# Three rounded products for the gated linear attention's far part, with its splits placed anew, and the last head's first gated sum ahead of two splits

## The chip, the cores and the metric

The kernel runs on one core of a Trainium2 chip. The metric is device time in microseconds of one execution; the time before is 752.98 us, the median of three runs (752.88 to 753.81). The profile shows five engines: PE (matrix products into PSUM; its weight loads are shown as PEld), DVE and ACT (elementwise work from PSUM and SBUF), POOL (elementwise work from SBUF) and SP (issues DMAs). Each engine works through its instructions in a fixed order and waits at an instruction until its inputs are there and the buffer it writes is free.

## The reference

One block of a model on 512 tokens of width 1024, in fp32: a root-mean-square norm, one wide projection, a gated linear attention of four heads (GLA), an attention of eight heads with low-rank queries and keys (MLA), a gated sum of both, an output projection, and an MLP with squared ReLU. What the change touches first is GLA's recurrence over chunks of 64 tokens, forward and backward:

```python
    def step(state, inp):
        qc, kc, vc, dc = inp
        o = jnp.einsum('bhck,bhkv->bhcv', qc, state)
        state = state * dc[..., None] + jnp.einsum('bhck,bhcv->bhkv', kc, vc)
        return state, o
```

and second the gated sum `merged = sigmoid(z_ma) * y_gla + sigmoid(z_mb) * y_mla` ahead of `merged @ w_out`.

## The kernel before

**Number format.** A product of fp32 precision is made of three products of rounded values: each operand is split into a high part `hi` (rounded, written by ACT as a copy) and a low part `lo` (the operand less `hi`, written by DVE, or by POOL if `split` is told so; lines 91 to 94). `mm3` (lines 87 to 90) issues hi·hi, hi·lo and lo·hi into the same accumulator. A few products are still plain fp32 matmuls: GLA's scores, and line 742.

**GLA.** The 512 tokens are four tiles of 128. For head h, `gla_scores` makes the scores within a tile and between the two tiles of a half, and splits them and the transposed keys kT (lines 566 to 573). What crosses from one half of the sequence to the other goes through a matrix of 128 × 512: `gla_state` (line 574) multiplies keys by values for both halves in twelve rounded products, and ACT copies the accumulator to SBUF (`gla0s` to `gla3s`, line 584). `gla_out` (line 728) then adds, for each tile i of queries, the scores times the values and, at line 742, the queries `far[:, 0, i]` times the matrix of the other half: four fp32 matmuls, which the profile records as eight. The queries in `far` were multiplied by POOL in the head before (line 512, `across`). `gla_squares`, `gla_gated` and, a head later, `gla_turn` norm, gate and transpose the result; the transposes land in PSUM and ACT takes them from there at line 776 (`yg`).

**A head's loop.** Heads 0 to 2 run in one loop. Beside GLA of head h it makes the gates of head h+1 (`Gates`: scans and differences on DVE, exponentials on ACT, small copies on POOL), multiplies queries and keys by them (`within` on DVE, `across` on POOL) and projects queries and keys of head h+2; `begin_qk` loads and splits a weight (gq2, gk2, gq3, gk3), `finish_qk` multiplies. In head 2 it is the projections ckv1, zb4 and zb5 instead. Head 3 stands behind the loop, beside the start of MLA: `ckv_.sums` and `ckv_.diagonals` norm the compressed keys (lines 807 to 815; the power at line 809 is on POOL), `rotary_k` turns the shared key on DVE (krsin, kswap, kr, lines 894 to 897), `rotary_begin` (line 864) loads and splits two weights wr0 and wr1, `rotary_k_split` copies kr to kbuf on ACT, two tanh and two `yg` follow on ACT, and PE makes the rotary queries (`up_T`, tiles ro0 and ro1) from wr0 and wr1.

**PSUM.** Accumulators come from two rings of four buffers, "at" and "mm"; a tile takes the buffer of the tile four before it in its ring and waits until that has been read. In "mm" the transposes of two `yg`, the spread of ckv's factors, ro0 and ro1 follow one another.

**The end of MLA.** Head 7 of MLA is the last. `att_values` (step n of a loop over 37 steps) multiplies probabilities by values, half of the tokens at a time; `merge` (line 1150) forms (gate + 1) × av on DVE (tile `tb`), and POOL adds the GLA part (`my`, line 1153). For the last head `merge` is called once for each half, and the av products of the second half, which write the same accumulator, wait until the first half has been read. The output projection splits sums of pairs of merged heads: `split_first` (gao) and `split_sum` (glyo, glzo); for the third pair their low parts are on DVE at steps 34 to 36.

**Order.** Within each engine the order of work is the scheduler's, from the emitted order and its readiness, fixed in places by explicit order: POOL's from the GLA loop on follows the emitted order (`in_program_order`), PE's and that of ACT and DVE do in large stretches, and `goes_behind` sets one group behind another on given engines.

Of the kernel before, what the change touches and what calls it, by code (L numbers as in the profile page):

```python
# [56 lines left out]
def tile_block(ctx: ExitStack, tc: tile.TileContext, t, out: bass.AP):  # L57
# [10 lines left out]
    def u2(name, dt=F32, shape=(P, S)):  # L68
        return tl(list(shape), dt, "u2", 29, name)

    def u4(name, dt=F32R, shape=(P, 2, S)):
        return tl(list(shape), dt, "u4", 26, name)
# [19 lines left out]
    def split(hi, lo, src, rest=nc.vector):  # L92
        nc.scalar.activation(hi, src, AF.Copy)  # L93
        rest.tensor_tensor(lo, src, raw(hi), op=ALU.subtract)  # L94
# [479 lines left out]
    def gla_state(h, keys):  # L574

        half, at = h // 2, (h % 2) * GDV
        c = slice(at, at + GDV)
        acc = ps("at", f"gla{h}st")
        for j in range(NT):
            tok = slice(j * P, (j + 1) * P)  # L580
            mm3(acc[:, (j // 2) * GDV : (j // 2 + 1) * GDV], keys[:, 0, tok], keys[:, 1, tok],
                v[j, half][:, 0, c], v[j, half][:, 1, c], j % 2 == 0, j % 2 == 1)
        state = u2(f"gla{h}s")
        nc.scalar.activation(state, acc, AF.Copy)
        return state

# [138 lines left out]
    def gla_out(h, sc, state, far):  # L727

        half, at = h // 2, (h % 2) * GDV
        accs = [ps("at", f"gla{h}o{g}") for g in range(2)]  # L730
        c = slice(at, at + GDV)
        os = [accs[i // 2][:, (i % 2) * GDV : (i % 2 + 1) * GDV] for i in range(NT)]
        for i, o in enumerate(os):
            g = i // 2
            for x in range(2):
                j = 2 * g + x
                tok = slice(x * 256 + (i % 2) * P, x * 256 + (i % 2 + 1) * P)
                mm3(o, sc[g][:, 0, tok], sc[g][:, 1, tok], v[j, half][:, 0, c], v[j, half][:, 1, c],
                    i % 2 == 0 and x == 0, False, True)
        for i, o in enumerate(os):  # L740
            other = 1 - i // 2
            nc.tensor.matmul(
                o, far[:, 0, i], state[:, other * GDV : (other + 1) * GDV], start=False, stop=True,
                skip_group_check=True,
            )
        return os

    def gla_squares(h, os):
# [115 lines left out]
    def rotary_begin():  # L864
        res = []
        for x in range(2):
            wf = stage(3, P, f"wr{x}")
            lo = NOPE + x * HALF
            for k in range(3):
                nc.sync.dma_start(  # L870
                    wf[:, k, :].rearrange("p (h e) -> p h e", h=MH), w_uq[:, k, :, lo : lo + HALF]
                )
            wh, wl = halves(3, P, f"wr{x}")
            split(wh, wl, wf)
            res.append((wh, wl))
        return res

# [289 lines left out]
    def begin_qk(h, x):  # L1167
        col, name = ((C_GQ, "gq"), (C_GK, "gk"))[x]
        return begin(col + h * P, f"{name}{h}")
# [87 lines left out]
    for h in range(GH - 1):  # L1257
        sc, keys, far = gla_scores(*scaled_qk.parts())
        scaled_qk = Scaled(h + 1)
        gate = Gates(h + 1)  # L1260
        gate.logs()
        latent, j = ((cq_, 1), (cq_, 2), (ckv_, 0))[h]
        acc = latent.products(j)
        if h < 2:
            w_b, lows = begin_late(C_GQ + (h + 2) * P, f"gq{h + 2}")
        else:
            ckv_.begun[1], lows = begin_late(C_CKV + P, "ckv1")
        (rotary.angles, rotary.reduced, cq_.diagonals)[h]()
        gate.sums("f")
        state = gla_state(h, keys)  # L1270
        gate.exps("f")
        lows()
        latent.keep(j, acc)
        gate.sums("b")
        gate.exps("b")
        scaled_qk.within("f", gate.parts)
        scaled_qk.across("f", gate.parts)
        if j:
            latent.add_squares()
        if h:  # L1280
            gla_turn(h - 1)
        os = gla_out(h, sc, state, far)
        scaled_qk.within("b", gate.parts)
        rs = gla_squares(h, os)
        scaled_qk.across("b", gate.parts)
        if h < 2:
            w_k = begin_qk(h + 2, 1)
            gla_gated(h, os, rs)
            finish_qk(h + 2, 0, w_b)
            if h == 0:  # L1290
                cq_.begin(2)
            else:
                ckv_.begin(0)
                cq_.sums()
            finish_qk(h + 2, 1, w_k)
        else:
            zb = begin(C_ZB + 4 * P, "zb4")
            gla_gated(h, os, rs)
            cq_.spread()
            ckv_.keep(1, ckv_.products(1))  # L1300
            ckv_.add_squares()
            w_b = begin(C_ZB + 5 * P, "zb5")
            zb = proj_run(zb, xT)

    h = GH - 1
    sc, keys, far = gla_scores(*scaled_qk.parts())
    ckv_.sums()
    zb5 = proj_run(w_b, xT)
    cq = cq_.normed()
    cos, sin = rotary.tables()  # L1310
    state = gla_state(h, keys)
    late = [over_rms(acc, f"b{f}") for f, acc in ((4, zb), (5, zb5))]
    ckv_.diagonals()
    rotary_k()
    wr = rotary_begin()
    zb = begin(C_ZB + 6 * P, "zb6")
# [46 lines left out]
    for n in range(4 * MH + LAG_C - 1):  # L1363
        if n % 2 == 0 and 2 <= n <= 4 * MH:
            att_normalise((n - 2) // 4, (n - 2) % 4)
        scored = traced()
        if n < 4 * MH:
            att_scores(n // 4, n % 4)
            if n - 2 in flipping:
                goes_behind((scored, traced()), flipping[n - 2], SPLITTERS)  # L1370
        scored = scored, traced()
        if n == 0:
            goes_behind(scored, last_gate, PE_ONLY)
        if n == 3:
            span["fourth"] = scored
        if 2 <= n % 8 < 7:
            at = traced()
            next(units, None)
            if n == 2:
                gla_turn(GH - 1)  # L1380
            if n < 4:
                goes_behind((at, traced()), scored, PE_ONLY)
        if n in (6, 14):
            units = up_units(n // 8 + 2)
            at = traced()
            next(units)
            if n == 6:
                goes_behind((at, traced()), span["fourth"], SPLITTERS[:1])
        b = n - LAG_B
        if n == 30:  # L1390
            xs_ = wo_accs[1] = [ps("mm", f"wox{rb}") for rb in range(2)]
            at = traced()
            wo_product(1, ps_=(0,))
            begun = at, traced()
            goes_behind(begun, scored, PE_ONLY)
        if 0 <= b < 4 * MH:
            flips = traced()
            att_flip(b // 4, b % 4)
            flipping[n] = flips, traced()
            if n == 30:  # L1400
                goes_behind(flipping[n], begun, PE_ONLY)

        if n == 20:
            load_onto(B11, B12, w_out)
        extra = traced()
        for x, at in (("y", (18, 26, 34)), ("z", (20, 28, 36))):
            if n in at:
                p = at.index(n)
                to = (5, 6) if x == "y" else (7, 3)
                split_sum(wo_left[p], sums_of[p, x], *to, f"{x}o{p}", nc.gpsimd if p < 2 else nc.vector)  # L1410
        if n in (19, 30):
            p = (19, 30).index(n)
            split_first(wo_left[p], merged[p][0], f"o{p}", nc.gpsimd)
        if n < 4 * MH:
            goes_behind((extra, traced()), scored, SPLITTERS[:1])
        if n == 35:
            split_first(wo_left[2], merged[2][0], "o2")
        if n in (11, 13):
            streamed(1, B11, (n - 11) // 2)
            split_streamed(1, (n - 11) // 2)  # L1420
        if n in (21, 23):
            streamed(2, B21, (n - 21) // 2)
        if n == 15:
            load_w2(0, B11, w_out)
        if n == 17:
            at = traced()
            load_w2(0, B21, w_out, B22)
            span["sums"] = at, traced()
        if n == 23:
            load_onto(B21, B11, w_out)  # L1430
        if n == 24:
            load_w2(0, B12, w_out)
            load_w2(0, B22, w_out)
        c = n - LAG_C
        if c >= 0 and c % 2 == 1:
            att_values(c // 4, (c % 4) // 2)
        if n == 33:
            load_onto(B21, B12, w_out)
        if c > 0 and c % 8 == 7 and c // 8 < NP - 1:
            sums_of[c // 8, "y"], sums_of[c // 8, "z"] = merged_sums(c // 8, nc.gpsimd)  # L1440
# [334 lines left out]
```

## Time and profile before

| | |
|---|---|
| time, median of 3 runs | 752.98 us (752.88 to 753.81) |
| profiled execution | 753.01 us, span 751.0 us |
| granted clock of PE, mean | 0.999 |
| PE busy | 741.9 us, 99% of the span |
| DVE / ACT / POOL busy | 581.4 / 457.5 / 166.0 us |
| data moved by DMA | 88.90 MB, mean 118 GB/s |

A line of a timeline gives the start in us from the start of the span, the duration in us, the engine, the line of the kernel, the operation, the tile written and the tiles read, and the shape. `xN` joins N instructions of one form. A bracket at the end gives how long the engine had been idle before the instruction and what ended that. PE's matmuls overlap at their ends: their spacing is the time that one takes, not the duration shown. In the chain of work that ended last a line has start, length, engine and tile. L93 is the high part of a split and L94 its low part, L88 to L90 are the three products of `mm3`, whichever tile they are for.

### The profile page before, as it was taken

What the parts mean: (1) busy time and instruction counts of PE and PEld (TensorE: products, weight loads), DVE (VectorE), ACT (ScalarE), POOL (GpSimd) and SP (SyncE); (2) the same over time, 40 slices, a digit from 0 to 9 for tenths busy, and PEclk for the clock granted to TensorE, in tenths of its full rate; (3) what the DMA queues carried; (4) which work ended last, traced back from release to release, by engine and by line L of the source; (5) the groups of instructions that cost most, each with busy time, mean ns of one, the idle gap of its engine ahead of it and who ended that gap; (6) DMA issues with size and microseconds to landing.
All of it is one profiled execution on the core that took longest, in us unless ns stands there. A gap on an engine that the chain in (4) does not pass through costs nothing.

```text
span 751.0 us, 10202 instructions
## 1 busy us (share of the span) xinstructions
PE 741.9 (99%) x3688; PEld 628.3 (84%) x3688; DVE 581.4 (77%) x842; ACT 457.5 (61%) x776; POOL 166.0 (22%) x238
## 2 busy tenths in 40 slices
PE   9999999999999999999999999999999999999996
PEld 7888888888889888899888988888888888888885
DVE  7777886989787587888897688857696578747795
ACT  8556574686577476887956765435644464445644
POOL 0722110252672521246740100000000000000014
PEclk9999999999999999999999999999999999999999
DMA  9859582611222243459698321551226310640003
GB/s 309 266 128 231 175 175 84 113 29 29 84 57 39 40 92 102 109 145 249 196 226 245 107 67 30 168 169 56 57 85 196 113 57 21 203 141 0 29 0 113
DMA packets 94722, 88.90 MB, mean 118 GB/s; under 512 B 15792, under 2 KB 66992, under 8 KB 94672
## 3 DMA queue, kind: packets, MB, share of 16 engines
q1 hardware_dynamic: 88176, 75.64, 33.5%
q0 software_dynamic: 6208, 12.32, 9.2%
q8 instruction: 29, 0.48, 0.3%
q10 hardware_dynamic: 288, 0.28, 0.1%
q14 instruction: 21, 0.17, 0.1%
HBM read 83.25 MB, written 2.10 MB: 114 GB/s over the span
## 4 chain that ended last, share of the span: by engine, by line
PE 98%; DVE 1%; issue 0%; POOL 0%; ACT 0%; POOLq 0%
PE f L88 8%; PE f L89 8%; PE f L90 8%; PE gx L88 4%; PE gx L89 4%; PE gx L90 4%; PE first L330 3%; PE gz L88 2%; PE gz L89 2%; PE gz L90 2%; PE tp L1122 2%; PE zb L88 1%; PE zb L89 1%; PE zb L90 1%; PE s L88 1%; PE s L89 1%
## 5 line engine op out<-in xcount | busy, mean ns | idle before, releaser
L1714 POOL DMA_DIRECT2D gfin<-in_g_final x1 | 0.6, 628 | 284.0 <-PE f L90 284.0
L977 DVE TENSOR_TENSOR w<-w,w 128x1024 f32<-128x1024 f32 x32 | 38.7, 1220 | 0.3
L1102 DVE TENSOR_REDUCE top<-s 128x1 f32<-128x512 f32 x32 | 21.8, 683 | 5.6 <-PE s L90 5.5
L1107 ACT ACTIVATE e<-s,top 128x512 f32<-128x512 f32 x32 | 22.0, 687 | 4.1 <-DVE top L1102 3.1
L94 DVE TENSOR_TENSOR pT<-tp,pT 128x512 fp32r<-128x512 f32 x32 | 21.8, 682 | 2.4 <-ACT pT L93 2.0
L1452 DVE TENSOR_TENSOR h<-h,gx 128x512 f32<-128x512 f32 x32 | 21.5, 681 | 1.9 <-PE gx L90 1.8
L93 ACT ACTIVATE pT<-tp 128x512 fp32r<-128x512 f32 x32 | 19.0, 595 | 3.2 <-PE tp L1122 3.2
L88 PE MATMUL av<-pT,v 128*128 128x256 f32 x64 | 19.2, 300 | 0.9 <-DVE tb L1150 0.9
L1122 PE MATMUL tp<-ident,e 128*128 128x128 f32 x128 | 19.4, 274 | 0.0
L93 ACT ACTIVATE ghb<-y 128x512 fp32r<-128x512 f32 x16 | 10.1, 632 | 14.0 <-DVE y L923 14.0
L1518 ACT ACTIVATE fa<-f 128x512 f32<-128x512 f32 x32 | 18.5, 577 | 0.0
L90 PE MATMUL av<-pT,v 128*128 128x256 f32 x64 | 18.2, 284 | 0.0
L89 PE MATMUL av<-pT,v 128*128 128x256 f32 x64 | 18.1, 283 | 0.0
L1122 PEld LDWEIGHTS tp<-ident,e 128*128 128x128 f32 x128 | 15.2, 140 | 3.1 <-ACT e L1113 0.6
L93 ACT ACTIVATE b_00h<-w 128x1024 fp32r<-128x1024 f32 x7 | 7.4, 1060 | 12.6 <-PE gz L90 6.0
L562 ACT ACTIVATE bds<-bd 128x512 f32<-128x512 f32 x4 | 2.4, 597 | 20.5 <-PE bd L545 20.5
L93 ACT ACTIVATE b_10h<-w 128x1024 fp32r<-128x1024 f32 x7 | 7.4, 1059 | 12.1 <-PE gz L90 6.0
L93 ACT ACTIVATE b_20h<-w 128x1024 fp32r<-128x1024 f32 x7 | 7.4, 1059 | 12.1 <-PE gz L90 6.0
L973 POOL DMA_DIRECT2D w<-in_w_out x10 | 12.4, 1428 | 7.6 <-DVE bo60l L94 6.5
L88 PE MATMUL s<-kbuf,q 96*128 96x512 f32 x32 | 14.1, 439 | 0.0
L1527 ACT ACTIVATE px<-fa 128x256 f32<-128x256 f32 x32 | 13.4, 418 | 1.0
L646 POOL DMA_DIRECT2D gvw<-in_w_in x4 | 4.8, 1226 | 38.7 <-DVE gvw L651 34.0
(1769 smaller groups left out, 2920.0 us busy)
## 6 DMA issues: line engine op xcount, KB each, us to landing
w<-in_w_ff SPq DMA_DIRECT2D x64, 256.0 KB, 3.4
w<-in_w_out POOLq DMA_DIRECT2D x10, 512.0 KB, 9.3
grw<-in_w_in SPq DMA_DIRECT2D x8, 512.0 KB, 9.1
zaw<-in_w_in SPq DMA_DIRECT2D x8, 512.0 KB, 6.7
gvw<-in_w_in SPq DMA_DIRECT2D x8, 512.0 KB, 4.6
w<-in_w_out SPq DMA_DIRECT2D x16, 256.0 KB, 5.6
x<-in_xt SPq DMA_DIRECT2D x8, 256.0 KB, 5.2
vw<-in_w_first SPq DMA_DIRECT2D x8, 256.0 KB, 5.4
```

The lines of the kernel that those rows point to most:

```text
L88: nc.tensor.matmul(acc, lh, rh, start=start, stop=False, skip_group_check=onto)
L89: nc.tensor.matmul(acc, lh, rl, start=False, stop=False, skip_group_check=onto)
L90: nc.tensor.matmul(acc, ll, rh, start=False, stop=stop, skip_group_check=onto)
L93: nc.scalar.activation(hi, src, AF.Copy)
L94: rest.tensor_tensor(lo, src, raw(hi), op=ALU.subtract)
L330: nc.tensor.matmul(f_accs[i], a[:, i * P : (i + 1) * P], b, start=k == 0 and x == 0, stop=k == KD - 1 and x == 2)
L977: nc.vector.tensor_tensor(wq[dst][g], wq[x][g], wq[y][g], op=op)
L1102: nc.vector.tensor_reduce(top, acc, axis=AX.X, op=ALU.max, negate=True)
L1107: nc.scalar.activation(e, acc, AF.Exp, bias=top, accum_out=tot[:, qt % 2 : qt % 2 + 1])
L1122: nc.tensor.transpose(tp[:, k * P : (k + 1) * P], e[:, k * P : (k + 1) * P], ident)
L1452: nc.vector.tensor_tensor(hc, hc, acc, op=op)
L1518: nc.scalar.activation(a, acc, AF.Relu)
```

## The change

- **Far part of GLA.** `gla_state` returns a split matrix (hi by ACT, lo by DVE) in place of one copy. A new function `far_queries` splits the 128 × 512 queries (tile `qF`, hi by ACT, lo by POOL). The four fp32 matmuls of each head become twelve rounded products.
- **Order in heads 0 to 2.** The splits of gk2 and gk3 (`begin_qk(h + 2, 1)`) stand ahead of `gla_out`: on ACT ahead of the squares of head h, on DVE ahead of the two multiplies of `within("b")`. qF's high part stands on ACT ahead of the copy of the matrix, its low part on POOL ahead of the small copies v3f.
- **Order in head 3.** qF is split right behind the scores: its low part stands on POOL ahead of the power at line 809. The matrix is split behind `over_rms` and the diagonals: its low part stands on DVE between the second diagonal and krsin.
- **wr0 and wr1.** Their low parts go from DVE (behind the last kr) to POOL (behind the power at line 809). On SP the load of zb7 now stands ahead of three copies of kbuf.
- **End of MLA.** At steps 34 to 36 the third pair's splits stand behind `att_values`, so that on DVE the gated sum `tb` of the first half of head 7 stands ahead of gao and glyo; glzo stood behind it before too.

```diff
@@ gla_state, far_queries
-        state = u2(f"gla{h}s")
-        nc.scalar.activation(state, acc, AF.Copy)
+        state = u4(f"gla{h}s")
+        split(state[:, 0, :], state[:, 1, :], acc)
         return state
+
+    def far_queries(far):
+
+        hl = u4("qF")
+        split(hl[:, 0, :], hl[:, 1, :], far[:, 0].rearrange("p a b -> p (a b)"), nc.gpsimd)
+        return hl
@@ gla_out
         for i, o in enumerate(os):
-            other = 1 - i // 2
-            nc.tensor.matmul(
-                o, far[:, 0, i], state[:, other * GDV : (other + 1) * GDV], start=False, stop=True,
-                skip_group_check=True,
-            )
+            other = slice((1 - i // 2) * GDV, (2 - i // 2) * GDV)
+            tok = slice(i * P, (i + 1) * P)
+            mm3(o, far[:, 0, tok], far[:, 1, tok], state[:, 0, other], state[:, 1, other], False, True, True)
         return os
@@ rotary_begin
-            split(wh, wl, wf)
+            split(wh, wl, wf, nc.gpsimd)
@@ heads 0 to 2
         gate.sums("f")
+        far = far_queries(far)
         state = gla_state(h, keys)
         gate.exps("f")
...
         if h:
             gla_turn(h - 1)
+        if h < 2:
+            w_k = begin_qk(h + 2, 1)
         os = gla_out(h, sc, state, far)
         scaled_qk.within("b", gate.parts)
         rs = gla_squares(h, os)
         scaled_qk.across("b", gate.parts)
         if h < 2:
-            w_k = begin_qk(h + 2, 1)
             gla_gated(h, os, rs)
@@ head 3
     sc, keys, far = gla_scores(*scaled_qk.parts())
+    far = far_queries(far)
     ckv_.sums()
     zb5 = proj_run(w_b, xT)
     cq = cq_.normed()
     cos, sin = rotary.tables()
-    state = gla_state(h, keys)
     late = [over_rms(acc, f"b{f}") for f, acc in ((4, zb), (5, zb5))]
     ckv_.diagonals()
+    state = gla_state(h, keys)
     rotary_k()
     wr = rotary_begin()
@@ end of MLA
-        for x, at in (("y", (18, 26, 34)), ("z", (20, 28, 36))):
+        for x, at in (("y", (18, 26)), ("z", (20, 28))):
...
-                split_sum(wo_left[p], sums_of[p, x], *to, f"{x}o{p}", nc.gpsimd if p < 2 else nc.vector)
+                split_sum(wo_left[p], sums_of[p, x], *to, f"{x}o{p}", nc.gpsimd)
...
-        if n == 35:
-            split_first(wo_left[2], merged[2][0], "o2")
...
         if c >= 0 and c % 2 == 1:
+            valued = traced()
             att_values(c // 4, (c % 4) // 2)
+            valued = valued, traced()
+        if n == 35:
+            at = traced()
+            split_first(wo_left[2], merged[2][0], "o2")
+            goes_behind((at, traced()), valued, SPLITTERS[1:])
+            split_sum(wo_left[2], sums_of[2, "y"], 5, 6, "yo2")
+        if n == 36:
+            split_sum(wo_left[2], sums_of[2, "z"], 7, 3, "zo2")
```

## The prediction

> **What bounds the kernel now.** I read the page first, then the chain of work that ended last, then the timelines of each engine around the places that the diff touches. From the page:
>
> ```profile
> span 751.0 us, 10202 instructions
> PE 741.9 (99%) x3688; PEld 628.3 (84%) x3688; DVE 581.4 (77%) x842; ACT 457.5 (61%) x776; POOL 166.0 (22%) x238
> PEclk9999999999999999999999999999999999999999
> PE 98%; DVE 1%; issue 0%; POOL 0%; ACT 0%; POOLq 0%
> ```
>
> PE carries 98% of the chain and its granted clock never drops. So the time is the sum of the matmuls plus whatever PE waits for; an edit on another engine counts only where it adds or removes a PE wait. I therefore take each edit twice: what it does to PE's own work, and how much slack it uses up ahead of PE. The sum is made against the profiled execution, 753.01 us (its span of 751.0 and 2.0 around it), which stands 0.03 above the median of the runs, 752.98. A difference within 0.2% (1.5 us) is about what a measurement of this kernel can't tell from no change.
>
> **Gain 1: queries times key-value matrix.** Four times (heads 0 to 3) four fp32 matmuls, recorded as eight, become twelve rounded products. Chain pieces of the first and last block, then the timeline of twelve rounded products of the same shape, the first one and the matmul after the twelfth:
>
> ```profile
> 187.57 1.73 PE gla0o L742 x8
> 270.05 1.73 PE gla3o L742 x8
> ...
> 183.09 0.28 PE L88 MATMUL gla0st<-gv,kT 128*128 128x256 f32 x1
> 184.52 0.28 PE L88 MATMUL gla0o<-gv,sc 128*128 128x256 f32 x1
> ```
>
> Twelve products take 184.52 − 183.09 = 1.43 us, the old block 1.73. Gain 0.30 per head, 1.2 in all. [...]
>
> **Gain 2: the last head's first gated sum.** The only recorded wait of PE behind its start is here. PE, then DVE, then the chain:
>
> ```profile
> 372.72 0.28 PE L90 MATMUL av<-pT,v 128*128 128x256 f32 x1
> 374.00 0.39 PE L90 MATMUL wox<-bo10h,gao 128*128 128x512 f32 x1
> 375.26 0.36 PE L88 MATMUL av<-pT,v 128*128 128x256 f32 x1 [0.87 <-DVE tb L1150]
> ...
> 372.25 0.69 DVE L94 TENSOR_TENSOR pT<-tp,pT 128x512 fp32r<-128x512 f32 x1
> 372.86 0.78 DVE L94 TENSOR_TENSOR gao<-mx,gao 128x512 fp32r<-128x512 f32 x1
> 373.55 1.23 DVE L94 TENSOR_TENSOR glyo<-yo,ghyo 128x512 fp32r<-128x512 f32 x1
> 374.71 0.41 DVE L1150 SCALAR_TENSOR_TENSOR tb<-tb,av 128x256 f32<-128x256 f32 x1
> ```
>
> The second half's av products wait until the gated sum tb has read the first half. Its input is done at 373.00, but DVE first does gao and glyo. With tb ahead of both, it runs at about 373.0 to 373.4 and PE goes on 0.23 behind 374.00, the spacing of these matmuls, at 374.23: gain 375.26 − 374.23 = 1.03 (0.87 if only the recorded idle goes). gao and glyo come 0.4 later, and the third split glzo was behind tb already; they feed wo products that PE reaches later, and with a second less of waiting ahead of them I price them at 0. If that cover is gone, they cost their 0.4.
>
> **Prices of the new splits.** One row each: a high part on ACT, a low part on DVE, low parts on POOL of 128x512 and of 128x384:
>
> ```profile
> 266.40 0.60 ACT L584 ACTIVATE gla3s<-gla3st 128x512 f32<-128x512 f32 x1 [0.37 <-PE gla3st L90]
> 260.08 0.68 DVE L94 TENSOR_TENSOR kT<-kt,kT 128x512 fp32r<-128x512 f32 x1
> 359.43 1.29 POOL L94 TENSOR_TENSOR glyo<-yo,ghyo 128x512 fp32r<-128x512 f32 x1 [0.28 <-ACT ghyo L93]
> 277.64 1.02 POOL L94 TENSOR_TENSOR wq0l<-wq0f,wq0h 128x384 fp32r<-128x384 f32 x1
> ```
>
> Per head ACT gains 0.60 (qF's high part; the state's is the old copy), DVE 0.60 to 0.68 (the state's low part), POOL 1.29 (qF's low part). POOL is idle most of the time, but it can hold DVE up. POOL rows and the DVE rows beside them:
>
> ```profile
> 25.64 0.75 POOL L604 TENSOR_TENSOR xy<-xy,x 128x256 f32<-128x256 f32 x1
> 346.50 1.69 POOL L94 TENSOR_TENSOR glzo<-zo,ghzo 128x512 fp32r<-128x512 f32 x1
> ...
> 25.70 1.23 DVE L292 TENSOR_TENSOR xdg<-ident,xrh 128x512 fp32r<-128x512 f32 x1
> 347.32 1.17 DVE L1114 TENSOR_SCALAR e<-e,tot 128x512 f32<-128x512 f32 x1
> 266.81 0.69 DVE L292 TENSOR_TENSOR ckvdg<-ident,ckvrl 128x512 fp32r<-128x512 f32 x1
> 267.52 0.48 DVE L894 TENSOR_SCALAR krsin<-sin,gvec 32x512 f32<-32x512 f32 x1
> ```
>
> xdg started just after POOL's xy and took 1.23; the same line with POOL idle took 0.69. e took 1.17 under glzo; a tensor_scalar of equal width took 0.48. In both the excess (0.54, 0.69) is about the rest of POOL's instruction. I take it that such a DVE instruction waits for the whole POOL one. [...]
>
> **Loss: head 3, PE's second rotary product.** This is where the slack is thinnest:
>
> ```profile
> 259.33 0.59 ACT L93 ACTIVATE kT<-kt 128x512 fp32r<-128x512 f32 x1
> 260.86 0.17 DVE L808 TENSOR_SCALAR ckvr<-ckvr 128x4 f32<-128x4 f32 x1
> 266.90 0.52 ACT L93 ACTIVATE wr0h<-wr0f 128x384 fp32r<-128x384 f32 x1
> 269.36 0.68 DVE L897 TENSOR_TENSOR kr<-kr,kswap 32x512 f32<-32x512 f32 x1
> 270.07 0.63 ACT L93 ACTIVATE kbuf<-kr 32x512 fp32r<-32x512 f32 x1 [1.30 <-DVE kr L897]
> 270.72 1.28 ACT L380 ACT_TABLE_LOAD   x1
> 272.01 1.15 ACT L380 ACTIVATE tb<-zb 128x512 f32<-128x512 f32 x2
> 273.07 1.25 ACT L776 ACTIVATE yg<-y,gla_gain 128x512 f32<-128x512 f32 x2
> 274.15 0.39 PE L88 MATMUL ro<-cqhl,wr1h 128*128 128x512 f32 x1
> ```
>
> PE's ro at 274.15 takes the PSUM bank that the first yg empties (four buffers in that ring). The two yg end at 274.32, the first some 0.6 earlier, at 273.7: slack 0.4. They stand on ACT behind kbuf, which waits for DVE's last kr (ends 270.04), a table load and two tanh, all back to back. So what DVE loses ahead of kr comes out of 0.4, and PE itself arrives 0.30 earlier by gain 1 of this head. Three things delay DVE:
> - The state's low part now stands ahead of krsin: 0.60 to 0.68. The two wr low parts that leave DVE stood behind kr and give nothing back here. Alone: 0.60 + 0.30 − 0.4 = stall 0.5.
> - wr0l and wr1l on POOL, 1.02 each, from wr0h's end, 267.42: to 269.5. DVE comes to krsin at 268.1, waits for wr0l (268.5), krsin to 269.0; wr1l then holds kswap to 270.0; kswap and two kr at 0.6 to 0.7 end at 271.8 to 271.9 instead of 270.04. Stall 1.8 + 0.3 − 0.4 = 1.7.
> - qF's low part on POOL: qF's high part follows kT on ACT, ends about 260.5, and the low part runs to 261.8. The tensor_scalar at 260.86 waits for it, about 0.8, and DVE has no idle time from there to kr. As ACT's work then starts later too, wr0l and wr1l run to 270.0 and part of their delay is the same time: kr ends at about 272.4. Stall 2.4 + 0.3 − 0.4 = 2.3.
>
> Bounds: 0.5 (POOL holds nobody up) and 2.9 (all three in full: 0.6 + 2 × 0.9 + 0.8, less the net 0.1 of slack, with 0.2 for the order in which DVE and POOL take turns). I take 2.3, as both shapes have rows that show the hold.
>
> **Heads 0 to 2, and the rest.** Tightest rows, DVE's split and PE's first use, in head 0 and head 2:
>
> ```profile
> 192.53 1.51 DVE L94 TENSOR_TENSOR gk2l<-gk2f,gk2h 128x1024 fp32r<-128x1024 f32 x1 [0.75 <-ACT gk2h L93]
> 195.07 0.39 PE L90 MATMUL gk<-xT,gk2l 128*128 128x512 f32 x1
> ...
> 247.54 1.23 DVE L94 TENSOR_TENSOR zb4l<-zb4f,zb4h 128x1024 fp32r<-128x1024 f32 x1 [2.57 <-ACT zb4h L93]
> 250.25 0.39 PE L90 MATMUL zb<-xT,zb4l 128*128 128x512 f32 x1
> ```
>
> gk2l ends at 194.04, 1.03 ahead of PE. It is moved ahead of two multiplies (0.68 each) that it no longer waits for, which pays for the state's 0.68 and most of a hold: 0. The multiplies come up to 1.5 later for POOL's products of the next head, which PE needs only in that head. zb4l isn't moved: slack 250.25 − 248.77 = 1.48, less 0.30 that PE gains, less about 0.7 (state) and up to 0.7 of hold: stall 0 to 0.4, I take 0.1. The load of zb7 ahead of three copies on SP's queue, and wq0 and wk0 which now wait for POOL's wr parts to free their staging buffers, are needed microseconds later: 0, and up to 1.0 (one POOL instruction) without that cover. In head 3 the pow of the ckv rows stands behind qF's low part on POOL; that is the 0.8 counted above.
>
> **Sum.** −1.2 − 1.03 + 2.3 + 0.1 = +0.2, 753.2 with both holds; with the wr holds alone −1.2 − 1.03 + 1.7 + 0 = −0.5, 752.5. I forecast 752.9, between them.
>
> **Rivals.**
> - A, the holds mostly don't happen: DVE's instructions slip in ahead, or qF's low part finds DVE in an instruction that it does not block. [...] Against: the four rows above. 753.01 − 2.23 + 0 to 0.5 = 750.8 to 751.3: faster. It decides below a stall of 0.7. Chance 0.30.
> - B, my forecast with one of the two holds or both: 753.01 − 2.23 + 1.7 to 2.5 = 752.5 to 753.3, the same. Chance 0.52 (with the range between A and B).
> - C, DVE's lateness reaches PE in heads 0 to 2 as well. Each head adds 0.68 and, if qF's low part takes 1.69 as under contention at 346.50, that hold to DVE. Head 2: 0.68 + 1.69 + 0.30 − 1.48 = 1.2; heads 0 and 1 some 0.3 each, as the moved gk split buys 1.36. With 753.1 that gives 754.3 to 754.9, slower from a stall of 1.5 in the three heads on. Against: ACT, not DVE, releases zb4l (2.57 of idle). Chance 0.18.
> - D, gain 1 fails, since weight loads or fp32 state pace the new products: +1.2, 754.2, inside "the same"; counted with B. [...]
>
> The range takes in A and most of C: 750.8 to 754.8; B's own is 752.2 to 753.6.
>
> **What would show it.** The gla0o block at 1.43 instead of 1.73 in all four heads. No wait of av for tb near 374, which otherwise refutes gain 2. A PE wait of about 2.3 us at the rotary products, ended by ACT's yg: none or 0.5 is A. Beside it the small tensor_scalar of ckvr at about 1.0 instead of 0.17, and krsin or kswap lengthened while POOL does wr0l or wr1l. No wait over 0.4 at zb4; over 1 is C. The clock row staying at 9. The forecast falls if the stall of head 3 is under 0.7, or if a wait appears at a place that I priced at 0.

## The result and the profile after

The changed kernel takes 755.99 us (median of 22 runs, 753.84 to 756.57), the kernel before 753.18 (22 runs, 752.88 to 754.03): ratio of the means 1.0027, 95% interval [1.002, 1.0033]; of the medians 1.0037. It is slower by 0.3 to 0.4%, where no change was forecast. Its executions fall into two groups 2.1 us apart, 9 at 753.84 to 754.35 with a mean granted clock of 0.997 or 0.998, and 13 at 755.75 to 756.57 with 0.995 or 0.996; the profiled one, 755.75, is of the second.

From the page of the changed kernel, and its waits of PE (us in total, times, longest):

```profile
span 754.0 us, 10250 instructions
PE 743.1 (99%) x3704; PEld 629.1 (83%) x3704; DVE 587.4 (78%) x844; ACT 459.5 (61%) x780; POOL 172.6 (23%) x244
PEclk9999999999999999999999999999999999999998
PE 91%; DVE 5%; issue 2%; ACT 1%; POOL 0%; POOLq 0%; DVEq 0%; ACTq 0%
...
PE ro L88 <- ACT yg L780: 2.0, 1, 2.0
PE warm L320 <- POOL ident masks.py:199: 1.5, 1, 1.5
PE wox L88 <- ACT f00h L93: 0.4, 1, 0.4
```

PE's wait for tb is gone, the wait of ro for yg is there, and a second, unforecast one has come at wox. The clock row still reads 9 (the 8 in its last slice lies behind PE's last product): a slice is 18.9 us, and what happens is shorter. Stretches around the wait show it (the stretch and its length in us, PE's busy time and products, granted clock, DMA share, GB/s):

```profile
270.50:272.90 2.40, 2.40 (x13) 1.00 0.75 184
272.90:275.20 2.30, 0.35 (x2) 1.00 0.49 121
275.20:278.60 3.40, 3.40 (x8) 0.53 0.80 195
278.60:281.00 2.40, 2.40 (x11) 0.95 0.00 0
```

Behind the wait PE runs at half its clock for some 3.4 us. The same in single products of PE, before, across and behind the wait:

```profile
272.86 0.39 PE L90 MATMUL ro<-cqhl,wr0l 128*128 128x512 f32 x1
275.20 0.63 PE L88 MATMUL ro<-cqhl,wr1h 128*128 128x512 f32 x1 [1.95 <-ACT yg L780]
275.63 0.63 PE L89 MATMUL ro<-cqhl,wr1h 128*128 128x512 f32 x1
278.62 0.50 PE L90 MATMUL ro<-cqhl,wr1l 128*128 128x512 f32 x1
278.96 0.39 PE L88 MATMUL zb<-xT,zb6h 128*128 128x512 f32 x1
```

From start to start the wait costs 275.20 − 272.86 − 0.23 = 2.1. The nine products behind it take 278.96 − 275.20 = 3.76 instead of 9 × 0.23 = 2.07: 1.7 more.

What made yg late, on DVE, POOL and ACT of the changed kernel:

```profile
260.12 0.97 DVE L812 TENSOR_SCALAR ckvr<-ckvr 128x4 f32<-128x4 f32 x1
267.46 0.68 DVE L94 TENSOR_TENSOR gla3s<-gla3st,gla3s 128x512 fp32r<-128x512 f32 x1
268.18 0.53 DVE L898 TENSOR_SCALAR krsin<-sin,gvec 32x512 f32<-32x512 f32 x1
268.75 1.39 DVE L899 TENSOR_TENSOR kswap<-kswap,krsin 32x512 f32<-32x512 f32 x1
270.77 0.68 DVE L901 TENSOR_TENSOR kr<-kr,kswap 32x512 f32<-32x512 f32 x1
...
259.78 1.28 POOL L94 TENSOR_TENSOR qF<-qk,qF 128x512 fp32r<-128x512 f32 x1 [5.81 <-ACT qF L93]
267.06 1.37 POOL L94 TENSOR_TENSOR wr0l<-wr0f,wr0h 128x384 fp32r<-128x384 f32 x1 [4.89 <-ACT wr0h L93]
268.39 1.20 POOL L94 TENSOR_TENSOR wr1l<-wr1f,wr1h 128x384 fp32r<-128x384 f32 x1
...
271.49 0.63 ACT L93 ACTIVATE kbuf<-kr 32x512 fp32r<-32x512 f32 x1 [3.14 <-DVE kr L901]
274.48 1.25 ACT L780 ACTIVATE yg<-y,gla_gain 128x512 f32<-128x512 f32 x2
```

The tensor_scalar of 128 × 4 values lasts until POOL is done with qF (261.06). kswap starts under POOL's wr1l, which is done at 269.59, and ends 0.55 behind it; in the kernel before, with POOL idle, it took 0.68. Meanwhile ACT stands idle for 3.14 us with two yg behind it that need nothing from DVE.

### The profile page after: what moved, and what is told of

Its sections match the earlier page's. It is cut to its first block, busy times and chain, and to the rows that moved or that the text cites. A ratio compares the mean times of both kernels' runs of the same rounds, so it can differ in the third digit from the quotient of the medians.

```text
span 754.0 us, 10250 instructions
## 1 busy us (share of the span) xinstructions
PE 743.1 (99%) x3704; PEld 629.1 (83%) x3704; DVE 587.4 (78%) x844; ACT 459.5 (61%) x780; POOL 172.6 (23%) x244
## 4 chain that ended last, share of the span: by engine, by line
PE 91%; DVE 5%; issue 2%; ACT 1%; POOL 0%; POOLq 0%; DVEq 0%; ACTq 0%
PE f L90 8%; PE f L88 8%; PE f L89 8%; PE gx L88 4%; PE gx L90 4%; PE gx L89 4%; PE first L330 3%; PE gz L90 2%; PE gz L88 2%; PE tp L1126 2%; PE gz L89 2%; PE zb L89 1%; PE zb L88 1%; PE zb L90 1%; PE s L88 1%
## 5 line engine op out<-in xcount | busy, mean ns | idle before, releaser
L94 POOL TENSOR_TENSOR qF<-qk,qF 128x512 fp32r<-128x512 f32 x4 | 6.6, 1640 | 38.6 <-ACT qF L93 38.6
```

## Experiments

Each kernel was measured beside the kernel before, whose median was 753.2 to 753.4 in these series. Four theories are at stake. G: the gain at the last head is given back, because DVE works with hardly a pause there (rival K: it is kept). S: the wait of ro is ACT's order behind a late kr, and the half clock is its result. W: the clock falls only behind a wait that is long enough. P: POOL's instructions hold DVE's up.

**The end of MLA alone**, put into the kernel before:

```diff
-        if n == 35:
-            split_first(wo_left[2], merged[2][0], "o2")
...
+        if n == 35:
+            at = traced()
+            split_first(wo_left[2], merged[2][0], "o2")
+            goes_behind((at, traced()), valued, SPLITTERS[1:])
+            split_sum(wo_left[2], sums_of[2, "y"], 5, 6, "yo2")
```

> The kernel before with only the end of MLA changed (tb ahead of gao and glyo). Theory G (the gain at the last head is given back): PE's wait near 374 goes, 1.0 us, but DVE works back to back behind it and decides when PE's products some 30 us later may start; a wait of PE for ACT or DVE appears near 409 and the time is 753.2 to 753.5 (0 to +0.3 on 753.2). Rival K (the gain is kept): 752.2, no new wait.

753.31 us, ratio 0.9998 [0.9989, 1.0007]: no change. The wait for tb is gone. One of DVE's long splits there (bo50l), and ACT's split of bo40, first in the kernel before, then with the end changed, and then the new wait:

```profile
380.11 1.21 DVE L94 TENSOR_TENSOR bo50l<-w,bo50h 128x1024 fp32r<-128x1024 f32 x1
404.61 1.04 ACT L93 ACTIVATE bo40h<-w 128x1024 fp32r<-128x1024 f32 x1
```

```profile
380.71 1.76 DVE L94 TENSOR_TENSOR bo50l<-w,bo50h 128x1024 fp32r<-128x1024 f32 x1
405.77 1.04 ACT L93 ACTIVATE bo40h<-w 128x1024 fp32r<-128x1024 f32 x1
408.81 0.47 PE L88 MATMUL wox<-bo40h,gdo 128*128 128x512 f32 x1 [0.32 <-ACT f00h L93]
```

This execution was 0.70 behind from its start (PE's first products). Against that, PE is 1.10 ahead behind the second half's av. DVE however is not ahead: bo50l ends at 382.47 instead of 381.32, 1.15 later, so 0.45 behind even with the 0.70 taken off. ACT's bo40h is 1.16 later as well. By the starts of the same products in both timelines PE loses 0.2 at 379, 0.6 around 409, where it has caught up with ACT and DVE, and 0.1 by 427; it goes through the MLP only 0.2 ahead. DVE is busy for 25.7 of the 26 us from 373 to 399 in the kernel before, and for 25.6 with the end changed, so it has nothing to catch up with. Theory G holds: 0.9 of 1.1 is given back.

**The changed kernel with the end of MLA as before** (the same lines, the other way round).

> The changed kernel with the end of MLA put back as before. Theory G: about as the changed kernel, 0 to 0.3 below it: 753.8 to 756.2 by the clock that is granted. Rival K: 1.0 slower than the changed kernel in the same clock, 755 to 757. In both the wait of ro for yg stays at 2.0 us.

756.12 us in six executions, two at 754.14 and 754.32 and four at 755.94 to 756.68: each group about where the changed kernel has it. The profiled one is of the first group, and its stretches beside those shown above say what sets the groups apart:

```profile
272.90:275.20 2.30, 0.34 (x2) 1.00 0.56 148
275.20:278.60 3.40, 3.40 (x16) 1.00 0.71 172
```

The wait is the same, the clock behind it is full. So the end of MLA changes next to nothing, and one and the same wait costs clock in some executions and none in others.

**The two yg first on ACT**, in the changed kernel:

```diff
+    gla_turn(h - 1)
     kbuf = rotary_k_split()
     g2 += [half_tanh(z, f"b{f}") for f, z in ((4, late[0]), (5, late[1]))]
-    gla_turn(h - 1)
```

> The changed kernel with the two yg of head 3 put ahead of kbuf and the two tanh on ACT; nothing else moves. Theory S (the 2.1 us wait of ro is ACT's order behind the late kr, and the half clock behind it is a result of that wait): the wait is 0, the granted clock 0.999 in all executions, the time 753.2 - 1.2 + 0.2 = 752.2 with theory G, 751.0 with rival K. Rival M (the wait moves on: kr is still late, so something else of MLA's start waits for kbuf or the tanh): a wait of 1 to 2 us at another tile within 20 us, time 753.5 to 755. Rival C (the lower clock does not hang on the wait): clock still 0.995 to 0.998, 754.

751.84 us in one group (751.68 to 752.39), ratio 0.9982 [0.9973, 0.9991]. ACT and PE of this kernel, and its waits:

```profile
268.10 1.25 ACT L780 ACTIVATE yg<-y,gla_gain 128x512 f32<-128x512 f32 x2
271.33 0.63 ACT L93 ACTIVATE kbuf<-kr 32x512 fp32r<-32x512 f32 x1 [1.99 <-DVE kr L901]
272.93 0.39 PE L88 MATMUL ro<-cqhl,wr1h 128*128 128x512 f32 x1
...
PE warm L320 <- POOL ident masks.py:199: 1.5, 1, 1.5
PE wox L88 <- ACT f00h L93: 0.3, 1, 0.3
```

DVE's chain is as late as before (kswap still 1.39), but nothing that PE needs hangs on it: no wait, no half clock, no second group. The mean clock is still 0.997 or 0.998 there, as in executions of the kernel before: it also holds the half clock behind PE's last product (here from 745.38 on, with that product done at 742.92), so a mean of that size says nothing. Against the changed kernel this one move of two ACT instructions is worth 4.2 us, and it is 1.4 faster than the kernel before. Theory S holds, rivals M and C fall.

**The same with the end of MLA as before.**

> As yg_first, and the end of MLA as before. What is left is the rounded products with their splits. Theory S with G: 753.2 - 1.2 = 752.0, within 0.3 of yg_first. With rival K: 752.0, and yg_first is 1.0 faster than this.

752.09 us (751.84 to 752.91), ratio 0.9989 [0.998, 0.9997]. What the rounded products are worth alone is thus 1.1, about what four times 0.30 had; the end of MLA adds at most 0.25, less than single executions of one kernel differ by. The same move of yg **in the kernel before**:

> The kernel before with the two yg of head 3 ahead of kbuf and the tanh. Theory S: no wait of ro to remove, so no change, 753.2. Rival (the order on ACT is itself worth something): below 752.7.

753.15 us, ratio 0.9999 [0.9991, 1.0008]: where nothing is late, the order on ACT is worth nothing.

**kr made late by nothing else**: in the kernel before, two, four or six more multiplies on DVE ahead of krsin, whose results are overwritten.

```diff
         sgn = u2("krsin")
+        for _ in range(4):
+            nc.vector.tensor_tensor(sgn, sin, cos, op=ALU.mult)
         nc.vector.tensor_scalar(sgn[r], sin[r], cst[r, K_SIGN : K_SIGN + 1], None, op0=ALU.mult)
```

> The kernel before with two more 128x512 multiplies on DVE ahead of krsin, whose results are overwritten: some 1.2 us that only make kr late. Theory S: kr late by 1.2 makes PE wait for yg by 1.2 - 0.4 = 0.8; theory W (the clock falls only behind a wait that is long enough, and 0.87 was not): clock row full, time 753.2 + 0.8 = 754.0. Rival (each wait costs clock in proportion): 754.7.

> As late2 with four multiplies: kr 2.4 late, PE's wait 2.0, like that of the changed kernel. Theory W: some executions at 753.2 + 2.0 = 755.2 with full clock and some at 757 with the clock halved for about 3.4 us behind the wait, the two groups 2.0 apart as in the changed kernel. Rival (the two groups of the changed kernel have another cause than this wait): one group at 755.2.

> As late2 with six multiplies: kr 3.6 late, PE's wait 3.2. Theory W: nearly every execution loses clock too, 753.2 + 3.2 + 1.7 or more = 758.1 or above, in one group. Rival: one group at 756.4 with full clock.

754.36 (754.07 to 755.18), 756.06 (755.54 to 756.43, five executions) and 759.48 us (six executions: 756.44, 757.08, and four at 759.39 to 759.98). PE's waits at the rotary products in the three, in this order:

```profile
PE ro L88 <- ACT yg L776: 0.8, 1, 0.8
```

```profile
PE ro L88 <- ACT yg L776: 1.2, 1, 1.2
PE ro L90 <- DVE wr0l L94: 0.8, 1, 0.8
```

```profile
PE ro L90 <- DVE wr0l L94: 2.2, 1, 2.2
PE ro L88 <- ACT yg L776: 0.9, 1, 0.9
```

The first has the wait that was worked out, 0.8, one group, and full clock in its trace. The time is 1.0 longer (ratio 1.0013), between the two that were expected, since from start to start the recorded 0.8 costs 0.98. The other two came out otherwise than expected: here wr0l is still on DVE behind kr, so it is late too, and the wait comes in two pieces. Four multiplies give 2.0 in sum, as expected, but no piece over 1.2, and there is one group where two were expected. Six give one piece of 2.2 and one of 0.9 instead of 3.2, and two groups where one was expected: four of six executions take some 2.9 longer than the other two.

**Only the wr low parts back on DVE**, and **only head 3's qF low part on DVE**, in the changed kernel:

```diff
-            split(wh, wl, wf, nc.gpsimd)
+            split(wh, wl, wf)
```

```diff
-    def far_queries(far):
+    def far_queries(far, rest=nc.gpsimd):
...
-    far = far_queries(far)
+    far = far_queries(far, nc.vector)
     ckv_.sums()
```

> The changed kernel with the low parts of wr0 and wr1 on DVE behind kr, as before. Theory P (POOL's instruction holds DVE's up): kswap 0.68 again instead of 1.39 and krsin 0.48 instead of 0.53, kr 0.75 earlier, PE's wait 2.0 - 0.75 = 1.25, the clock mostly full, time about 754.1 - 0.75 = 753.4 in most executions. Rival (POOL holds nobody up, kswap waits for something else): kr as late as in the changed kernel, wait 2.0, 754 to 756.

> The changed kernel with the low part of head 3's qF on DVE instead of POOL. Theory P: the tensor_scalar of ckvr is back from 0.97 to 0.17, DVE takes on 0.60 to 0.68 for qF itself, so kr comes 0.1 to 0.2 earlier: PE's wait 1.8 to 1.9, time within 0.3 of the changed kernel in each clock group (753.8 to 754.1, 755.6 to 756). Rival (POOL's qF costs DVE nothing): kr 0.6 later, wait 2.6, 754.7 or more.

With the wr low parts on DVE, 753.09 us (752.88 to 753.97, one group), ratio 0.9999. kswap and PE's wait:

```profile
268.68 0.68 DVE L899 TENSOR_TENSOR kswap<-kswap,krsin 32x512 f32<-32x512 f32 x1
274.44 0.50 PE L88 MATMUL ro<-cqhl,wr1h 128*128 128x512 f32 x1 [1.16 <-ACT yg L780]
```

With qF's low part on DVE, 753.84 us, nine executions at 753.54 to 754.44 and two at 756.2:

```profile
259.78 0.68 DVE L94 TENSOR_TENSOR qF<-qk,qF 128x512 fp32r<-128x512 f32 x1
260.57 0.17 DVE L812 TENSOR_SCALAR ckvr<-ckvr 128x4 f32<-128x4 f32 x1
274.85 0.50 PE L88 MATMUL ro<-cqhl,wr1h 128*128 128x512 f32 x1 [1.75 <-ACT yg L780]
```

Theory P holds in both: kswap is back at 0.68 with POOL out of its way, the small tensor_scalar at 0.17. POOL's wr parts cost 0.8 of the wait; its qF part costs DVE 0.80, about what the split itself costs there (0.68), so moving it there frees only 1.95 − 1.75 = 0.2.

Put side by side by the longest single wait of PE in this place, taken from the one profiled execution of each kernel, the executions that by their times lost the clock: 0.8 us none of 11, 1.2 none of 11 and none of 5, 1.7 two of 11, 2.0 to 2.1 thirteen of 22 and four of 6, 2.2 four of 6.

What decides within a group stands in the traces. The granted clock changed in them at steps of 3.413 us. In the changed kernel it falls at 275.42, rises one step later at 278.84, and falls again behind PE's last product at 749.88, 471.04 us or 138 steps further on; with six multiplies it falls at 277.29, rises two steps later at 284.12, and falls at 755.16, again 471.04 us or 138 steps further on. Without a fall near the wait the steps can be counted back from the fall at the end (749.13 for the changed kernel with the end of MLA as before, 749.53 with qF's low part on DVE), taken as even. Where they lie in the program differs between the traces: one stands at 275.42 in the changed kernel and one at 274.68 with the end as before, with PE's wait at the same place in both. Stretches from step to step around the wait, columns as above, of the changed kernel, of six multiplies, of the end as before, and of qF's low part on DVE:

```profile
272.01:275.42 3.41, 1.46 (x7) 1.00 0.63 183
275.42:278.84 3.42, 3.42 (x9) 0.50 0.73 172
...
273.88:277.29 3.41, 1.35 (x6) 1.00 0.08 15
277.29:280.70 3.41, 2.53 (x7) 0.50 0.79 197
280.70:284.12 3.42, 3.42 (x9) 0.50 0.97 221
...
271.27:274.68 3.41, 1.83 (x9) 1.00 0.54 156
274.68:278.09 3.41, 3.04 (x13) 1.00 0.88 223
...
271.67:275.08 3.41, 1.66 (x8) 1.00 0.62 187
275.08:278.50 3.42, 3.42 (x16) 1.00 0.67 166
```

In these traces the fall goes with how long PE was busy between two steps. Half clock followed stretches at full clock with 1.46 us of PE (changed kernel) and 1.35 (six multiplies), and at the end of the program with 0.44 (changed kernel, 746.46 to 749.88) and 0 (kernel before, 746.07 to 749.48). It did not follow those with 1.62 (kernel before, 742.65 to 746.07), 1.66 (qF's low part on DVE), 1.83 (the end as before) and 2.54 (kernel before, 374.01 to 377.42, with its wait for tb). So theory W holds in another form: the same wait of 2.0 costs clock where it falls between two steps, and not where a step cuts it (into 1.6 and 0.4 in the traced execution with the end as before). If the steps fall evenly, a wait of 1.95 lies whole between two in (3.41 − 1.95) / 3.41 = 43% of executions, an estimate, and in some more nearly whole; 17 of 28 lost the clock. With four multiplies none of 5 lost it: at most 1.5 of the two waits fits into 3.41 us, which leaves 1.9 of PE. Six lose 2.9, not 1.7, because the second wait lies in the half clock: that stretch has 2.53 of PE, and another at half clock follows it. Why two of 11 executions with a wait of some 1.7 lost the clock stays open, as neither was traced.

## Why the prediction was wrong

- **Gain 1: right.** With yg first PE comes to wr1's first product at 272.93 instead of 274.15, 1.2 ahead after four blocks, 0.30 for each.
- **Prices and the hold of POOL: right in kind.** The tensor_scalar took 0.97 where "about 1.0" was forecast, and kswap 1.39. krsin was hardly lengthened (0.53), so the 0.4 that wr0l was to cost there fell away.
- **The loss at ro: right place, nearly right size.** 2.3 forecast, 2.1 measured. Of this, the wr parts are 0.8 where the step had 1.2 (1.7 less 0.5), qF's part on POOL is 0.8 (the 0.2 freed and the 0.6 that DVE took on) where it had 0.6, and 0.5 is left for the state's low part, as it had; this last is a remainder, no run moved that part alone.
- **Heads 0 to 2: right.** No wait at zb4; rival C did not occur. That the time came out slower is not by C's way.
- **The step that failed first: "a PE wait of about 2.3" was costed at its own length.** The sum had no term for what PE does behind the wait, though the clock row was named as something to watch, and that row is too coarse to show it. The half clock costs 1.7 more in the profiled execution and, by their times, in 13 of 22, and that takes the median to 756.0, out of the range.
- **The step that failed second: "I price them at 0"** for gao and glyo behind tb. The cover that was named, slack of wo products that PE reaches later, was looked for one tile at a time. DVE has only some 0.3 of pause in 26 us from there, so it was as much the limit of that stretch as PE. Its work did not shrink, and it even ended 0.45 later: beside POOL's instructions some of its splits took longer (glzo 1.22 instead of 0.68, bo50l 1.76 instead of 1.21) and one less long (bo21l 1.21 instead of 2.10). That POOL is the reason is not tested here. Of 1.03, 0.2 is left.

With the measured terms the sum comes out: 753.18 − 1.2 − 0.2 + 2.1 = 753.9 for the group with full clock (753.84 to 754.35), and 755.6 with 1.7 more (755.75 to 756.57), short of the groups' means by 0.2 and 0.6. Executions differ by as much without any of this: the 22 of the kernel before lie 1.15 apart (752.88 to 754.03). Less the 1.7, the median would be 754.4, inside the range, and the slowest execution 754.9, just above it.

## What to carry to other kernels

A PE wait isn't worth its own length only: if it, or several close together, may leave PE busy for no more than about 1.5 of 3.41 us (here half clock came behind 1.46 and not behind 1.62), add a chance of half clock behind it, and look at stretches of 2 or 3 us, since the row of 40 slices doesn't show it and the mean doesn't show it reliably. When a wait goes away, ask which engine had no pause around it; if another worked back to back there, the gain lasts until PE meets that engine again. And where an in-order engine idles on a late input, look at what is queued behind that could have gone first: two ACT instructions moved into a gap of 3 us turned a loss of 2.8 into a gain of 1.4.

## What the runs showed of the hardware

- The granted clock changed at steps of 3.413 us, whose place in the program differed between the traces (275.42 in the changed kernel, 274.68 with the end of MLA as before). It fell to 0.50 behind stretches between two steps with 1.46 us (changed kernel) and 1.35 us of PE (six multiplies), and not behind those with 1.62 (kernel before), 1.66 (qF's low part on DVE) and 1.83 (the end as before). It stayed there for 3.41 us behind one wait of 1.95 in the changed kernel, and for 6.83 with six multiplies, where a second wait left PE busy for 2.53 us of the first stretch at half clock. With four multiplies, waits of 0.8 and 1.2 with seven products between them did not bring it down.
- A tensor_scalar over 128 × 4 values took 0.97 us in the changed kernel, beside POOL's subtraction of two 128 × 512 tiles, and 0.17 with that subtraction on DVE; a 32 × 512 multiply took 1.39 beside POOL's 128 × 384, and 0.68 with that on DVE.
